# A seven-product scheme for part of the feed forward's first product

## The chip, the cores and the metric

The kernel runs on one core of a Trainium2 chip. The metric is the device time of one execution in microseconds; the kernel before takes 2246.73 us (median of 3 runs, 2246.26 to 2246.96).

## The reference, cut to what matters

Two transformer layers over 256 tokens of width 2048 in float32. The change is in the first layer's feed forward, whose hidden width is 5632:

```python
def swiglu(x, w_in, w_out):
    g, u = jnp.split(x @ w_in, 2, axis=-1)
    return (jax.nn.silu(g) * u) @ w_out
```

Here `w_in` is [2048, 11264], its left half the gate, its right half the up projection. Ahead of it stand a mixer and an attention over a memory, each with a residual and a layer norm; behind it a residual, a layer norm and the second layer.

## The kernel before, in words

Every large product is taken with TensorE in float32r. A float32 operand is written as the sum of a high part, the operand rounded to float32r, and a low part, the rest. `split` (L100) makes them: ScalarE copies to the high part (L101), VectorE subtracts it from the operand for the low part (L102). `mm3` (L121) takes a product as three matmuls: high by high (L124), activations' high by weights' low (L125), activations' low by weights' high (L126). The activations are stationary, one tile of 128 rows by 128 tokens; the weights move, 512 columns at a time, so one block of 128 rows by 512 columns costs three matmuls for each of the two token tiles.

`load_w` (L105) loads a chunk of weights in pieces of 2 blocks of 128 rows (128 x 1024 numbers, 512 KB) on SyncE's queue (SP, L112) into a `raw` tile, and splits it into a `hi` and a `lo` tile. Each of these pools has six tiles. `gemm_panels` (L128) goes through a panel of 512 columns block by block, both token tiles per block, and calls `evac` when a PSUM tile is complete.

The feed forward's first product is done by `ffn_in(j)` for j from 0 to 10 (L606 to L624). Each is a double panel: 512 columns of the gate, with silu on ScalarE (L611), then 512 columns of the up projection; VectorE multiplies (L619), and `to_pair` transposes the product with TensorE (L165) and splits it into `hT[j]`. For j = 0, the gain and offset of the second layer norm are applied to x (L556, L557) with bias tiles that GpSimd (POOL) loads (L93). The inner dimension of 2048 is 16 blocks of 128 rows. The second product follows in groups of 4, 4 and 3 double panels (L632), the first double panel of the next group being done ahead of it. PSUM's eight banks are 4 for products (`ps_g`), 2 for transposes (`ps_t`), 2 for attention (`ps_a`).

The kernel is written with a framework that sets the order of each engine's instructions and gives out the tiles of a pool at build time, by the order of the program and by when it reckons that an instruction is ready; on the chip each engine then runs its list in order. So a wait for a tile's release is a wait for the last reader of the tile before it.

Of the kernel before, what the change touches and what calls it, by code (L numbers as in the profile page):

```python
# [29 lines left out]
HEAD = 8  # L30
# [5 lines left out]
# columns of w_in  # L36
# [4 lines left out]
def build(ctx, tc, nc, a):  # L41
# [11 lines left out]
    stat = pool("stat", 4)  # L53
    ps_g = pool("ps_g", 4, PSUM)
    ps_t = pool("ps_t", 2, PSUM)
    ps_a = pool("ps_a", 2, PSUM)
# [20 lines left out]
    # token tile 1 sees 256 keys; the tables of tile 0 are the right halves of its  # L77
# [27 lines left out]
    def load_w(chunk_ap, kn, n, pieces=1):  # L105
        """One chunk of weights: kn blocks of 128 rows, n columns; hi and lo parts of each."""
        parts = []
        for k0 in range(0, kn, 2):
# [6 lines left out]
            for i in range(pieces):  # L115
                q = slice(2 * i // pieces, 2 * (i + 1) // pieces)
                split(raw[:, q, :], hi[:, q, :], lo[:, q, :])
# [36 lines left out]

    def acts_of(pairs):
        return [(h[:, i, :], l[:, i, :]) for h, l in pairs for i in range(4)]
# [4 lines left out]
    def transpose4(src):  # L161
        """src [128, 512] -> PSUM [128, 4, 128], each block of 128 columns transposed."""
        pt = ps_t.tile([128, 4, 128], F32, name="ps_t", tag="ps_t")
# [31 lines left out]
    def scores(q, k, tt, w):  # L195
        ps = ps_a.tile([128, 2, 256], F32, name="ps_a", tag="ps_a")
# [19 lines left out]
    def weigh(ps, v, causal_keys=True):  # L216
        """ps: per token tile [128, 2, 256]; v(i, sc) -> [128 keys, 128]. PSUM [128, 2, 256] = out^T."""
        o = ps_a.tile([128, 2, 256], F32, name="ps_a", tag="ps_a")
        for i in range(2):
            pt = ps_t.tile([128, 4, 128], F32, name="ps_t", tag="ps_t")  # L220
# [83 lines left out]
    kvg = const.tile([128, 256], F32, name="kvg")  # L304
    bcast_load(kvg, a["kv_norm_g"], 256)
    kig = const.tile([128, 64], F32, name="kig")
    bcast_load(kig, a["idx_k_norm_g"], 64)
    kib = const.tile([128, 64], F32, name="kib")
    bcast_load(kib, a["idx_k_norm_b"], 64)

    cTh = const.tile([128, 2, 256], F32R, name="cTh")
    cTl = const.tile([128, 2, 256], F32R, name="cTl")
# [3 lines left out]
    def ev_misc(tt, ps):  # L316
# [21 lines left out]
        pt = ps_t.tile([128, 4, 128], F32, name="ps_t", tag="ps_t")  # L338
# [17 lines left out]
    # keys of the memory  # L356
# [3 lines left out]
    # indexer scores and the choice of 64 keys  # L360
    mdsa = []
    for tt in range(2):
        w = 128 * (tt + 1)
        acc = later(f"score{tt}", FLOOR, tt=tt)
        for bp in range(4):
            # blocks 2 bp, 2 bp + 1 of two heads each; the heads of one row half share a bank
            for half in range(2):
                pr = slice(64 * half, 64 * half + 64)
                ps = ps_a.tile([128, 2, 256], F32, name="ps_a", tag="ps_a")
# [19 lines left out]
    # keys and values of the latent attention, per head  # L389
# [113 lines left out]
    # residual + layer norm  # L503
# [16 lines left out]
    # gains and offsets of the layer norms with one column per block of 128 of x's columns  # L520
# [380 lines left out]
def _lay_out(i):  # L901
    f = {k: np.asarray(v) for k, v in i.items()}
    w = f["w_in"][0]
    o = {}
# [58 lines left out]
```

## Time and profile before

| | |
|---|---|
| median of 3 runs | 2246.73 us |
| span of the profiled execution | 2244.9 us |
| TensorE busy | 2217.8 us (99%), 10080 matmuls |
| VectorE busy | 1278.9 us (57%) |
| ScalarE busy | 1056.4 us (47%) |
| mean granted TensorE clock | 0.997 of full speed |
| bytes moved by DMA | 423.96 MB, 189 GB/s on average |

The span runs from the first to the last instruction of the one execution that was profiled; the runs' own times lie 1.8 us above it. Times of instructions below are from that execution. Matmuls overlap in their pipeline, so the time from one start to the next counts, not the listed duration.

### The profile page before, as it was taken

Reading aid. Unit: us, or ns where it says so; the run is one execution under the profiler, and the core shown is the slowest. Engines: PE = TensorE matmul, PEld = TensorE weight load, DVE = VectorE, ACT = ScalarE, POOL = GpSimd, SP = SyncE. Lnnn points to the kernel's source line nnn. Section 1 sums busy time; section 2 is a strip of 40 time slices with the busy share of each in tenths; the row PEclk is TensorE's granted clock in tenths of the full one; section 3 lists DMA queues with packets and bytes.
Section 4 is the critical chain, followed back from the end, with each engine's and each line's share of the span. In section 5 each row is a group of like instructions: output and inputs, shape, how many; then the busy total and the mean of one; then the engine's idle time right before and its main releaser. Section 6 shows DMA issues by size and latency. Waiting matters only on the chain.

```text
span 2244.9 us, 26525 instructions
## 1 busy us (share of the span) xinstructions
PE 2217.8 (99%) x10080; PEld 1819.9 (81%) x10080; DVE 1278.9 (57%) x1563; ACT 1056.4 (47%) x1327; POOL 36.8 (2%) x75
## 2 busy tenths in 40 slices
PE   8999999999999999999999999999999999999999
PEld 6788888888887788888888888887788888888887
DVE  5666455555558774454455545467565565655553
ACT  5655445444435554443344434446555554444442
POOL 1000000000000000000000000001000000000000
PEclk9999999999999999999999999999999999999999
DMA  7654555656766375555555556557455556666563
GB/s 275 206 166 144 183 174 171 200 194 199 249 196 197 132 236 191 191 188 192 193 188 188 190 194 194 187 173 229 144 173 175 165 169 203 197 204 199 191 201 115
DMA packets 118480, 423.96 MB, mean 189 GB/s; under 512 B 13728, under 2 KB 14288, under 8 KB 118352
## 3 DMA queue, kind: packets, MB, share of 16 engines
q1 hardware_dynamic: 113760, 407.59, 55.2%
q0 software_dynamic: 4592, 14.68, 2.4%
q8 instruction: 79, 1.29, 0.2%
q14 instruction: 49, 0.40, 0.1%
HBM read 420.11 MB, written 2.10 MB: 188 GB/s over the span
## 4 chain that ended last, share of the span: by engine, by line
issue 66%; PE 30%; DMA 2%; POOL 1%; DVE 1%; ACT 0%; POOLq 0%; DVEq 0%; ACTq 0%
PE ps_g L125 9%; PE ps_g L126 9%; PE ps_g L124 9%; DMA bb<-ln_b 1%; PE ps_t L165 1%; DMA bb<-ln_g 1%; POOL bb L93 0%; DMA bb<-b_gate 0%; PE ps_a L198 0%; PE ps_a L232 0%; DVE lo L102 0%; PE ps_a L233 0%; ACT tmp L298 0%; PE ps_t L221 0%; PE ps_a L741 0%
## 5 line engine op out<-in xcount | busy, mean ns | idle before, releaser
L102 DVE TENSOR_TENSOR lo<-raw,hi 128x1024 fp32r<-128x1024 f32 (+2 forms) x766 | 931.7, 1218 | 874.7 <-ACT hi L101 873.7
L101 ACT CAST hi<-raw 128x1024 fp32r<-128x1024 f32 (+2 forms) x766 | 802.5, 1049 | 1038.4 <-PE ps_g L126 995.9
L125 PE MATMUL ps_g<-lo,hnTh 128*128 128x512 f32 x768 | 301.8, 393 | 2.3 <-DVE lo L102 2.3
L126 PE MATMUL ps_g<-hi,hnTl 128*128 128x512 f32 x768 | 302.1, 393 | 0.0
L124 PE MATMUL ps_g<-hi,hnTh 128*128 128x512 f32 x768 | 302.1, 393 | 0.0
L124 PE MATMUL ps_g<-hi,x2Th 128*128 128x512 f32 x704 | 275.0, 391 | 0.0
L126 PE MATMUL ps_g<-hi,x2Tl 128*128 128x512 f32 x704 | 274.8, 390 | 0.0
L125 PE MATMUL ps_g<-lo,x2Th 128*128 128x512 f32 x704 | 274.2, 390 | 0.0
L124 PE MATMUL ps_g<-hi,xTh 128*128 128x512 f32 (+1 forms) x608 | 236.5, 389 | 6.2 <-ACT hi L101 6.2
L125 PE MATMUL ps_g<-lo,xTh 128*128 128x512 f32 (+1 forms) x608 | 236.9, 390 | 1.5 <-DVE lo L102 1.3
L126 PE MATMUL ps_g<-hi,xTl 128*128 128x512 f32 (+1 forms) x608 | 237.8, 391 | 0.0
L125 PEld LDWEIGHTS ps_g<-lo,hnTh 128*128 128x128 f32 x768 | 145.1, 189 | 32.3 <-DVE lo L102 2.7
L124 PEld LDWEIGHTS ps_g<-hi,hnTh 128*128 128x128 f32 x768 | 145.2, 189 | 29.7 <-ACT crow L742 0.3
L126 PEld LDWEIGHTS ps_g<-hi,hnTl 128*128 128x128 f32 x768 | 144.9, 189 | 29.5
L125 PEld LDWEIGHTS ps_g<-lo,x2Th 128*128 128x128 f32 x704 | 132.2, 188 | 27.3 <-DVE lo L102 0.2
L124 PEld LDWEIGHTS ps_g<-hi,x2Th 128*128 128x128 f32 x704 | 132.2, 188 | 27.2 <-DVE x2Th L546 0.2
L126 PEld LDWEIGHTS ps_g<-hi,x2Tl 128*128 128x128 f32 x704 | 132.2, 188 | 27.1
L124 PEld LDWEIGHTS ps_g<-hi,xTh 128*128 128x128 f32 x608 | 114.7, 189 | 28.9 <-ACT hi L101 6.9
L126 PE MATMUL ps_g<-hi,hTl 128*128 128x512 f32 x352 | 137.3, 390 | 0.0
L124 PE MATMUL ps_g<-hi,hTh 128*128 128x512 f32 x352 | 137.2, 390 | 0.0
L125 PE MATMUL ps_g<-lo,hTh 128*128 128x512 f32 x352 | 136.9, 389 | 0.0
L125 PEld LDWEIGHTS ps_g<-lo,xTh 128*128 128x128 f32 x608 | 114.6, 188 | 25.6 <-DVE lo L102 3.4
(325 smaller groups left out, 2403.3 us busy)
## 6 DMA issues: line engine op xcount, KB each, us to landing
raw<-w_fi SPq DMA_DIRECT2D x176, 512.0 KB, 4.1
raw<-w_qkvg SPq DMA_DIRECT2D x96, 512.0 KB, 3.7
raw<-w_g SPq DMA_DIRECT2D x96, 512.0 KB, 4.4
raw<-w_fo SPq DMA_DIRECT2D x88, 512.0 KB, 3.7
raw<-w_out SPq DMA_DIRECT2D x64, 512.0 KB, 4.5
raw<-w_ga SPq DMA_DIRECT2D x32, 512.0 KB, 4.7
raw<-w_gb SPq DMA_DIRECT2D x32, 512.0 KB, 4.6
raw<-w_up SPq DMA_DIRECT2D x24, 512.0 KB, 4.6
```

What stands on the lines that cost most here:

```text
L101: nc.scalar.copy(hi, src)
L102: nc.vector.tensor_sub(lo, src, hi.bitcast(F32))
L124: nc.tensor.matmul(ps, ah[:, tok(tt)], wh, start=first, stop=False)
L125: nc.tensor.matmul(ps, ah[:, tok(tt)], wl, start=False, stop=False)
L126: nc.tensor.matmul(ps, al[:, tok(tt)], wh, start=False, stop=last)
L165: nc.tensor.transpose(pt[:, i, :], src[:, i * 128:(i + 1) * 128], ident)
```

## The change

For the double panels 1 to 10, gate and up projection are done together in `duo`. The 16 blocks of rows are eight pairs. With the two token tiles, the two blocks of a pair and the two panels, a pair is a product of 2 x 2 blocks by 2 x 2 blocks. For pairs 0, 1 and 2 (`FAST`) it is taken with seven block products instead of eight (`seven`): `sums_of` makes four sums of activation blocks once, VectorE makes four sums of weight blocks each time, and these are split as well. Four of the seven products are gathered in PSUM over the three pairs and combined by `combine` into an addend for each of the four results; the other three go directly into the results' PSUM tiles. The remaining five pairs are done as before (`eight`), the last two together, token tile by token tile. In pairs 4, 5 and 7 (`BY_DMA`) the up projection's low part comes another way: ScalarE writes minus the high part, and a DMA on POOL's queue adds the weights to it. The order of the pairs is `PLAN`. `to_pair` is put off to the next double panel, behind `combine`.

With that go: transposes and attention share four PSUM banks (`ps_m`), some constants move from their own tiles into the pool of `unit` tiles, and the second product goes in groups of 3, 3, 3 and 2 double panels.

```diff
+PLAN = (0, 3, 1, 4, 2, 5, 6, 7)
+FAST = (0, 1, 2)
+BY_DMA = (4, 5, 7)
+FFN_GROUPS = ((0, 3), (3, 6), (6, 9), (9, 11))
...
+    hi1s = pool("hi1s", 2)
+    lo1s = pool("lo1s", 2)
     ps_g = pool("ps_g", 4, PSUM)
-    ps_t = pool("ps_t", 2, PSUM)
-    ps_a = pool("ps_a", 2, PSUM)
+    ps_m = pool("ps_m", 4, PSUM)
...
+    def split_dma(src, hi, lo):
+        nc.scalar.copy(hi, src)
+        nc.scalar.mul(lo, src, -1.0)
+        nc.gpsimd.dma_start(lo, src, accum_op=OP.add)
+    def load_w(chunk_ap, kn, n, pieces=1, by=None):
...
-                split(raw[:, q, :], hi[:, q, :], lo[:, q, :])
+                (by or split)(raw[:, q, :], hi[:, q, :], lo[:, q, :])
...
+    def sums_of(pr, q):
+        full = tmps.tile([128, 2, 256], F32, name="sfull", tag="tmp")
+        nc.vector.tensor_add(full, pr[0][:, 2 * q:2 * q + 2, :].bitcast(F32), pr[1][:, 2 * q:2 * q + 2, :].bitcast(F32))
+        z = tmps.tile([128, 4, 128], F32, name="ssum", tag="tmp")
+        a11, a21 = full[:, 0, tok(0)], full[:, 0, tok(1)]
+        a12, a22 = full[:, 1, tok(0)], full[:, 1, tok(1)]
+        nc.vector.tensor_sub(z[:, 0, :], a21, a22)
+        nc.vector.tensor_sub(z[:, 1, :], z[:, 0, :], a11)
+        nc.vector.tensor_sub(z[:, 2, :], a11, a21)
+        nc.vector.tensor_add(z[:, 3, :], a12, z[:, 1, :])
+        u = unit([128, 2, 4, 128], F32R, "sums")
+        split(z, u[:, 0], u[:, 1])
+        return [(u[:, 0, i, :], u[:, 1, i, :]) for i in range(4)]
+    later_q = []
+    def flush():
+        while later_q:
+            later_q.pop(0)()
+    def mm3s(ps, act, w, first, last):
+        (ah, al), (wh, wl) = act, w
+        nc.tensor.matmul(ps, ah, wh, start=first, stop=False)
+        nc.tensor.matmul(ps, ah, wl, start=False, stop=False)
+        nc.tensor.matmul(ps, al, wh, start=False, stop=last)
+    def duo(w0, w1, evacs, acts, sums, plan):
+        n = 512
+        aps = [w0, w1]
+        P = [[ps_g.tile([128, n], F32, name="ps_g", tag="ps_g") for _ in range(2)] for _ in range(2)]
+        used = [[0, 0], [0, 0]]
+        fast = [i for i in plan if i in sums]
+        slow = [i for i in plan if i not in sums]
+        extra = len(fast)
+        total = [[2 * len(slow) + extra, 2 * len(slow) + extra], [2 * len(slow) + extra, 2 * len(slow)]]
+        N = {}
+        def at(i, k, tt):
+            h, l = acts[2 * i + k]
+            return h[:, tok(tt)], l[:, tok(tt)]
+        def block(p, i, k):
+            j = 2 * i + k
+            return aps[p][j // 4].rearrange("p (k n) -> p k n", n=n)[:, j % 4, :]
+        def into(tt, p, act, w):
+            used[tt][p] += 1
+            mm3s(P[tt][p], act, w, used[tt][p] == 1, used[tt][p] == total[tt][p])
+        def raw_tile():
+            return raws.tile([128, 2, n], F32, name="raw", tag="raw")
+        def two(src):
+            h = his.tile([128, 2, n], F32R, name="hi", tag="hi")
+            l = los.tile([128, 2, n], F32R, name="lo", tag="lo")
+            split(src, h, l)
+            return (h[:, 0, :], l[:, 0, :]), (h[:, 1, :], l[:, 1, :])
+        def seven(i):
+            ra, rb = raw_tile(), raw_tile()
+            nc.sync.dma_start(ra[:, 0, :], block(0, i, 0))
+            nc.sync.dma_start(rb[:, 0, :], block(1, i, 0))
+            nc.sync.dma_start(ra[:, 1, :], block(1, i, 1))
+            nc.sync.dma_start(rb[:, 1, :], block(0, i, 1))
+            t13, t24 = raw_tile(), raw_tile()
+            b11, b22 = two(ra)
+            nc.vector.tensor_add(t13, ra, rb[:, 0:1, :].to_broadcast([128, 2, n]))
+            t1, t3 = two(t13)
+            nc.vector.tensor_add(t24[:, 0, :], t13[:, 0, :], ra[:, 1, :])
+            h = hi1s.tile([128, n], F32R, name="hi1", tag="hi1")
+            l = lo1s.tile([128, n], F32R, name="lo1", tag="lo1")
+            split(rb[:, 1, :], h, l)
+            nc.vector.tensor_add(t24[:, 1, :], t24[:, 0, :], rb[:, 1, :])
+            t2, t4 = two(t24)
+            if not N:
+                for m in ("1", "5", "7", "6"):
+                    N[m] = ps_m.tile([128, n], F32, name="ps_m", tag="ps_m")
+            s1, s2, s3, s4 = sums[i]
+            a, z = i == fast[0], i == fast[-1]
+            mm3s(N["1"], at(i, 0, 0), b11, a, z)
+            mm3s(N["5"], s1, t1, a, z)
+            mm3s(N["7"], s3, t3, a, z)
+            into(0, 0, at(i, 1, 0), (h, l))
+            into(0, 1, s4, b22)
+            mm3s(N["6"], s2, t2, a, z)
+            into(1, 0, at(i, 1, 1), t4)
+        def eight(group):
+            w = {}
+            for i in group:
+                for p in range(2):
+                    ap = aps[p][i // 2].rearrange("p (k n) -> p k n", n=n)[:, 2 * (i % 2):2 * (i % 2) + 2, :]
+                    w[i, p] = load_w(ap, 2, n, by=split_dma if p == 1 and i in BY_DMA else None)
+            for tt in range(2):
+                for p in range(2):
+                    for i in group:
+                        for k in range(2):
+                            into(tt, p, at(i, k, tt), w[i, p][k])
+                    if used[tt][p] == total[tt][p]:
+                        finish(tt, p)
+        add = {}
+        def combine():
+            e0 = unit([128, 2, n], F32, "add")
+            e1 = unit([128, 2, n], F32, "add")
+            add[0, 0], add[0, 1], add[1, 0], add[1, 1] = e0[:, 0, :], e0[:, 1, :], e1[:, 0, :], e1[:, 1, :]
+            nc.scalar.copy(add[0, 0], N["1"])
+            nc.vector.tensor_add(add[1, 0], add[0, 0], N["6"])
+            nc.vector.tensor_sub(add[0, 1], N["5"], add[1, 0])
+            nc.vector.tensor_add(add[1, 0], add[1, 0], N["7"])
+            nc.vector.tensor_sub(add[1, 1], N["5"], add[1, 0])
+        def finish(tt, p):
+            if add:
+                nc.vector.tensor_add(add[tt, p], add[tt, p], P[tt][p])
+                evacs[p](tt, add[tt, p])
+            else:
+                evacs[p](tt, P[tt][p])
+        rest, flushed = list(plan), False
+        while rest:
+            i = rest.pop(0)
+            if i in sums:
+                seven(i)
+                if i == fast[-1]:
+                    combine()
+                    flush()
+                    flushed = True
+            elif len(rest) <= 1:
+                eight([i] + rest)
+                rest = []
+            else:
+                eight([i])
+                if not fast and not flushed:
+                    flush()
+                    flushed = True
...
-        pt = ps_t.tile([128, 4, 128], F32, name="ps_t", tag="ps_t")
+        pt = ps_m.tile([128, 4, 128], F32, name="ps_t", tag="ps_m")
...
+    norms = unit([128, 384], F32, "norms")
+    kvg, kig, kib = norms[:, 0:256], norms[:, 256:320], norms[:, 320:384]
...
+    x2S = {}
...
-        gemm(a["w_fi"][2 * j], x2A, ev_g, head=HEAD if j == 0 else 0)
         hT[j] = pair("hT")
         def ev_u(tt, ps):
             nc.vector.tensor_mul(sg[tt], sg[tt], ps)
-            to_pair(sg[tt], hT[j], tt)
-        gemm(a["w_fi"][2 * j + 1], x2A, ev_u)
+            later_q.append(lambda: to_pair(sg[tt], hT[j], tt))
         if j == 0:
+            gemm(a["w_fi"][0], x2A, ev_g, head=HEAD)
+            gemm(a["w_fi"][1], x2A, ev_u)
+            flush()
             ln_affine(1)
+            for i in FAST:
+                x2S[i] = sums_of(x2T[i // 2], i % 2)
+        else:
+            duo(a["w_fi"][2 * j], a["w_fi"][2 * j + 1], (ev_g, ev_u), x2A, x2S, PLAN)
...
-    groups = [range(0, 4), range(4, 8), range(8, 11)]
+    groups = [range(j0, j1) for j0, j1 in FFN_GROUPS]
...
             ffn_in(groups[gi + 1][0])
+        flush()
...
-    for gi, (k0, k1) in enumerate(((0, 2048), (2048, 4096), (4096, 5632))):
-        o[f"w_fo{gi}"] = _panels(fo[k0:k1])
+    for gi, (k0, k1) in enumerate(FFN_GROUPS):
+        o[f"w_fo{gi}"] = _panels(fo[512 * k0:512 * k1])
```

## Rows read from the trace of the kernel before

**Rows 1.** The page's first part: engine, busy us (share of span), instructions.

```profile
span 2244.9 us, 26525 instructions
...
PE 2217.8 (99%) x10080; PEld 1819.9 (81%) x10080; DVE 1278.9 (57%) x1563; ACT 1056.4 (47%) x1327; POOL 36.8 (2%) x75
```

**Rows 2.** Busy time in stretches: feed forward, double panels 1 to 3, double panel 0.

```profile
core 0: us, PE busy (x) PEld busy (x) DVE busy (x) ACT busy (x) POOL busy (x), PEclk, DMA share, GB/s
836.00:967.00 131.00, 131.00 (x591) 108.43 (x590) 64.78 (x59) 56.23 (x60) 0.00 (x0) 1.00 0.59 189
790.00:1512.00 722.00, 721.63 (x3232) 596.61 (x3230) 377.73 (x363) 305.50 (x320) 4.53 (x8) 1.00 0.59 193
792.86:836.00 43.14, 43.14 (x196) 35.70 (x195) 31.46 (x36) 19.65 (x22) 3.77 (x7) 1.00 0.78 265
```

**Rows 3.** Waits, 740 to 1540 us: who waited for whom, us, times, longest.

```profile
ACT hi L101 <- PE ps_g L126: 416.7, 254, 5.7
DVE lo L102 <- ACT hi L101: 345.2, 250, 3.0
...
PEld ps_t L165 <- DVE sg L619: 2.8, 11, 0.3
```

**Rows 4.** Timeline of PE: a matmul and the twelfth after it.

```profile
880.41 0.39 PE L124 MATMUL ps_g<-hi,x2Th 128*128 128x512 f32 x1
...
883.13 0.39 PE L124 MATMUL ps_g<-hi,x2Th 128*128 128x512 f32 x1
```

**Rows 5.** Timeline of ACT: the silu of two double panels that follow each other.

```profile
890.13 1.28 ACT L611 ACTIVATE sg<-ps_g 128x512 f32<-128x512 f32 x2 [0.98 <-PE ps_g L126]
...
934.63 1.28 ACT L611 ACTIVATE sg<-ps_g 128x512 f32<-128x512 f32 x2 [0.98 <-PE ps_g L126]
```

**Rows 6.** Groups of instructions, 740 to 1540 us: busy us, mean ns, idle before.

```profile
L102 DVE TENSOR_TENSOR lo<-raw,hi 128x1024 fp32r<-128x1024 f32 x280 | 342.2, 1224 | 345.3 <-ACT hi L101 345.2
L101 ACT CAST hi<-raw 128x1024 fp32r<-128x1024 f32 x283 | 298.5, 1056 | 418.1 <-PE ps_g L126 416.7 <-ACT prob L584 0.8 <-ACT hi L101 0.3
...
L619 DVE TENSOR_TENSOR sg<-sg,ps_g 128x512 f32<-128x512 f32 x22 | 14.1, 680 | 0.0
...
L101 ACT CAST hTh<-ps_t 128x512 fp32r<-128x512 f32 x22 | 12.8, 582 | 0.9
```

**Rows 7.** Timeline of DVE: start, us, instructions that follow without a gap.

```profile
792.86 5.84 DVE L102 TENSOR_TENSOR lo<-raw,hi 128x1024 fp32r<-128x1024 f32 x5
...
825.82 1.28 DVE L102 TENSOR_TENSOR hTl<-ps_t,hTh 128x512 fp32r<-128x512 f32 x2
```

**Rows 8.** SP's loads at line 112: ns of an issue, min/median/max.

```profile
L112 SPq DMA_DIRECT2D raw<-w_fi x176: 327/328/328, 740.7 to 1412.4; - x176
```

**Rows 9.** DMA issues of the whole run: count, KB each, median us to landing.

```profile
raw<-w_fi SPq DMA_DIRECT2D x176, 512.0 KB, 4.1
...
bb<-ln_g POOLq DMA_DIRECT2D x12, 256.0 KB, 5.6
bb<-ln_b POOLq DMA_DIRECT2D x12, 256.0 KB, 5.1
...
x<-x POOLq DMA_DIRECT2D x4, 512.0 KB, 11.1
out<-x SPq DMA_DIRECT2D x8, 256.0 KB, 4.0
...
raw<-w_qi SPq DMA_DIRECT2D x4, 256.0 KB, 5.7
...
rb<-rel POOLq DMA_DIRECT2D x1, 512.0 KB, 9.3
```

**Rows 10.** Timeline of POOL, 798 to 1523 us: first, sixth, last two.

```profile
799.60 0.54 POOL L93 DMA_DIRECT2D bb<-ln_g  x1 [8.27 <-DVE x L557]
...
812.21 0.54 POOL L93 DMA_DIRECT2D bb<-ln_b  x1 [0.67 <-DVE x L556]
816.36 0.54 POOL L93 DMA_DIRECT2D bb<-ln_g  x1 [3.61 <-DMA bb<-ln_g]
1521.00 0.54 POOL L93 DMA_DIRECT2D bb<-ln_b  x1 [704.11 <-DVE x L556]
```

**Rows 11.** Busy time in stretches: x being loaded, bias tiles being loaded.

```profile
586.00:590.00 4.00, 4.00 (x20) 3.30 (x19) 2.28 (x2) 1.25 (x2) 0.00 (x0) 1.00 1.03 414
805.00:815.00 10.00, 10.00 (x45) 8.26 (x44) 7.34 (x10) 3.77 (x4) 1.61 (x3) 1.00 0.78 261
```

More of the change, by code (lines that the diff above doesn't have):

```diff
@@ L102, in split @@
         nc.vector.tensor_sub(lo, src, hi.bitcast(F32))
-    def load_w(chunk_ap, kn, n, pieces=1):
+    def split_dma(src, hi, lo):
[3 more added lines that the diff above has]
+    def load_w(chunk_ap, kn, n, pieces=1, by=None):
         parts = []
@@ new lines, in build @@
+    later_q = []
[107 more added lines that the diff above has]
+                    flushed = True
+        return
@@ L195, in scores @@
     def scores(q, k, tt, w):
-        ps = ps_a.tile([128, 2, 256], F32, name="ps_a", tag="ps_a")
+        ps = ps_m.tile([128, 2, 256], F32, name="ps_a", tag="ps_m")
         for i in range(2):
@@ L216, in weigh @@
     def weigh(ps, v, causal_keys=True):
-        o = ps_a.tile([128, 2, 256], F32, name="ps_a", tag="ps_a")
+        o = ps_m.tile([128, 2, 256], F32, name="ps_a", tag="ps_m")
         for i in range(2):
-            pt = ps_t.tile([128, 4, 128], F32, name="ps_t", tag="ps_t")
+            pt = ps_m.tile([128, 4, 128], F32, name="ps_t", tag="ps_m")
             nc.tensor.transpose(pt[:, 0, :], ps[0][:, i, 0:128], ident)
@@ L302, in build @@
     xA = acts_of(xT)
-    kvg = const.tile([128, 256], F32, name="kvg")
+    norms = unit([128, 384], F32, "norms")
+    kvg, kig, kib = norms[:, 0:256], norms[:, 256:320], norms[:, 320:384]
     bcast_load(kvg, a["kv_norm_g"], 256)
-    kig = const.tile([128, 64], F32, name="kig")
     bcast_load(kig, a["idx_k_norm_g"], 64)
-    kib = const.tile([128, 64], F32, name="kib")
     bcast_load(kib, a["idx_k_norm_b"], 64)
-    cTh = const.tile([128, 2, 256], F32R, name="cTh")
-    cTl = const.tile([128, 2, 256], F32R, name="cTl")
+    cT = unit([128, 4, 256], F32R, "cT")
+    cTh, cTl = cT[:, 0:2, :], cT[:, 2:4, :]
     kidxT = const.tile([128, 256], F32, name="kidxT")
@@ L337, in ev_misc @@
                                            op0=OP.mult, op1=OP.add)
-        pt = ps_t.tile([128, 4, 128], F32, name="ps_t", tag="ps_t")
+        pt = ps_m.tile([128, 4, 128], F32, name="ps_t", tag="ps_m")
         for i in range(3):
@@ L368, in build @@
                 pr = slice(64 * half, 64 * half + 64)
-                ps = ps_a.tile([128, 2, 256], F32, name="ps_a", tag="ps_a")
+                ps = ps_m.tile([128, 2, 256], F32, name="ps_a", tag="ps_m")
                 for i in range(2):
@@ L701, in build @@
     pick = fb[:, 2:4, :].rearrange("p a (b c) -> p (a b) c", c=128)
-    ps = ps_a.tile([4, 256], F32, name="ps_a", tag="ps_a")
+    ps = ps_m.tile([4, 256], F32, name="ps_a", tag="ps_m")
     for tt in range(2):
@@ L705, in build @@
     nc.vector.tensor_copy(r3row, ps)
-    ps = ps_a.tile([4, 256], F32, name="ps_a", tag="ps_a")
+    ps = ps_m.tile([4, 256], F32, name="ps_a", tag="ps_m")
     for k in range(16):
@@ L728, in build @@
     for tt in range(2):
-        ps = ps_a.tile([128, 4], F32, name="ps_a", tag="ps_a")
+        ps = ps_m.tile([128, 4], F32, name="ps_a", tag="ps_m")
         nc.tensor.transpose(ps, fz[:, tok(tt)], ident[0:4, 0:4])
@@ L738, in build @@
     for hp in range(2):
-        ps = ps_a.tile([128, 2, 256], F32, name="ps_a", tag="ps_a")
+        ps = ps_m.tile([128, 2, 256], F32, name="ps_a", tag="ps_m")
         for i in range(2):
```

## The prediction, made before the changed kernel was run

> **What bounds the kernel now.** I read the page's busy times first [rows 1]: TensorE (PE) is busy for 2217.8 of 2244.9 us, VectorE (DVE) for 57% and ScalarE (ACT) for 47%. The stretches by stage [rows 2] put the feed forward at 790 to 1512 us, where PE never stops; in nearly three double panels (836 to 967 us) DVE works 64.78 of 131 us and ACT 56.23. The waits of this stage [rows 3] say the same from the other side: ACT waits for a matmul to free a high-part tile (416.7 us), DVE waits for ACT's high part (345.2 us), and PE's own waits are a few us (its weight loads wait 2.8 us for the products that are transposed). So only PE time counts here, as long as the others keep up. One matmul of 512 columns follows the last every 2.72 / 12 = 0.2267 us (twelve lie between the two lines of [rows 4]); its listed 0.39 us overlaps. The gate's silu comes every 934.63 - 890.13 = 44.50 us [rows 5]: 192 matmuls (43.53), which leaves 0.12 us for each of 8 transposes.
>
> **What is removed.** A fast pair takes 21 matmuls instead of 24. Three pairs in each of 10 double panels save 90 matmuls: 90 x 0.2267 = 20.4 us, from 44.5 to 42.5 us a double panel. It is on the path, since PE bounds. The stationary tiles of the sums are 128x128 like the others. The median of the runs is 2246.7, 1.8 above the span of the profile; I take differences off the median, so 2226.3 is the whole gain.
>
> **What DVE gets.** Alone a 128x1024 subtraction takes 1.224 us and a 128x512 one 0.68 [rows 6]; back to back the pitch is (5.84 - 1.22) / 4 = 1.155 and about 0.60 [rows 7]. A fast pair has three wide low parts and one wide addition, one narrow low part and two narrow additions: 4 x 1.155 + 3 x 0.60 = 6.42 us. Three make 19.3. The five slow pairs have ten low parts, of which three go to DMA: 7 x 1.155 = 8.1. Combining takes 4 narrow operations, finishing 4, the product with the gate 2, the low parts of hT 2: 12 x 0.60 = 7.2. Sum 34.5 us, or 37.6 by the lone durations, against 41.5 us of matmuls: 83 to 91%, from 22 us before. It fits in the order of the plan too: pieces 0, 3, 1, 4, 2 need 19.3 + 3 x 1.155 = 22.7 us of DVE and give PE 3 x 4.76 + 2 x 5.44 = 25.2. ACT gets thirteen wide copies or negations of slow pairs (13.7), three fast pairs of 3 x 1.056 + 0.58 (11.2), one copy of a product, two silus and two hT parts (2.9): 27.8 us, which PE hides.
>
> **What the two chains add.** Inside a fast pair the chain is addition, ACT copy, subtraction, twice. The six slots of raw and of hi now serve 22 and 19 tiles a double panel instead of 16 each. PE's demand leaves room, because a slot of hi is taken again only after the last matmul of the tile before it. Loads come in 12 pieces of 256 KB and 10 of 512 KB; SP's issues are 0.33 us each [rows 8], 22 of them 7.3 of 41.5 us. A 512 KB weight load lands after 4.1 us; the 256 KB rows from SP are 4.0 and 5.7 [rows 9]. Between no cost and 1 us a panel I take 0.2 (the load fits before the need by my count): 2 us in all.
>
> **The accumulating DMA** is the open price; the trace has none. First its deadline. From the start of a double panel PE takes 4.76, 5.44, 4.76, 5.44, 4.76, 5.44 and 10.88 us. Pair 4's up weights are the tenth of the 19 hi tiles; with six slots, in order of need, they get the fourth to come free, pair 3's gate weights, last used at 4.76 + 0.75 x 5.44 = 8.84. They are first needed at 14.96 + 1.36 = 16.32. That leaves 7.48 us; ACT's copy and negation take 2 x 1.056 and the handovers about 0.2, so 5.2 us remain from issue to landing. For pair 5 it is the same (19.04 to 26.52). Pair 7 has 9.52 us, 7.2 net. A later landing stops PE, which runs in order, once each for pairs 4 and 5. Behind a waiting accumulation on POOL's queue stand only the next ones: the bias tiles are loaded up to 816 and from 1521 us [rows 10], the wait in between is on a free tile and costs nobody.
>
> Its price by rows [rows 9]: below, the quickest median of 256 KB, 4.0 us from SP (no stall); above, four loads of x issued together, 11.1 us (5.9 + 5.9 + 3.9 late, 157 us in all), and the first of two loads of rb, 9.3. Nearest are single POOL transfers beside weight traffic: the bias tiles, 256 KB, 5.1 and 5.6. They are half as long, but read the destination of nothing; 256 KB at the 414 GB/s seen when the queues are full [rows 11] are 0.6 us. On the other side, they fell into stretches with the transfers' engines 0.78 busy at 261 GB/s, where the feed forward otherwise has 0.59. I take 5.5: 0.3 late, 20 times, 6 us. For this transfer DMA: Bandwidth & Descriptors (the Trainium skill, section Bandwidth) gives 6.15 us of DMA time for 1 MB issued from GpSimd; half of it and the fixed 2 us of that page make an estimate of 5.1 us, by which this term would be nothing and the sum 2229. No run here shows it.
>
> Does DVE hold POOL's transfers up? The bias loads issued from 799.60 to 812.21 us [rows 10] went out between subtractions and additions on DVE, at 0.54 us each. SBUF — State Buffer (the Trainium skill, section Who interferes with whom) says that a DVE copy or cast in a two-port mode keeps GpSimd from writing descriptors until it ends, and that an operation with two SBUF inputs does not. By that nothing changes here, since the new DVE work has two inputs throughout; were descriptors held for a whole DVE instruction, 1.2 us would come on top, which is the slow rival's price below.
>
> **Once, and elsewhere.** Three sums after the first double panel: 3 x 6 operations of at most 0.60 = 10.8 us of DVE, which is busy for 31.46 of 43.14 us there [rows 2]; 0 to 3, I take 1. One more group of second products: 8 additions more on DVE of 0.68, hidden by PE; what covered the group's last hT before (the next group's first panel) still stands. Transposes and attention now share four PSUM banks instead of two and two: outside the feed forward PE idles about 27 us in all [rows 1], so -3 to +4; I take 0. The row norms' constants move pools: nothing.
>
> Sum: 2246.7 - 20.4 + 6 + 2 + 1 = 2235.3.
>
> **The rivals.**
> - *The whole gain.* Accumulations land within 5.2 us and the chains cost nothing: 2226. For it: PE has no wait in this stage, and weight loads land in 4.1 us [rows 9]. Against it: POOL's medians are longer than SP's.
> - *DVE becomes the bound.* If DVE idles for ACT's copy of both sums in each fast pair, 2 x 1.1 x 3 = 6.6 us a panel come on top of its 37.6 by the lone durations: 44.2 against 42.5, 1.7 lost in each of 10 panels: 2226.3 + 17 + 3 = 2246, no change. For it: DVE already waits for ACT before nearly every low part [rows 3]. Against it: other low parts are ready then, and the order of an engine's instructions is laid out by readiness.
> - *The accumulating DMA is late.* Issue to landing takes 6.7 us: 1.5 us late at pairs 4 and 5, 3 us a double panel, 30 in all: 2246.7 - 20.4 + 30 + 3 = 2259, slower. The balance turns at 5.2 + 17.4 / 20 = 6.1 us. For it: the 512 KB transfers on POOL's queue have medians of 9.3 and 11.1 us [rows 9], and an accumulation reads twice; its transfers and the weights share the queues' engines, busy 0.59 already [rows 2]. Against it: those rows were issued in groups.
>
> **How the numbers follow.** My sum (2235) gets 0.48, the whole gain 0.13, DVE bound 0.13, a late DMA 0.26. A measurement of this kernel tells about 0.2% (4.5 us) from no change. The sum and the whole gain lie on the faster side: 0.61; DVE bound is the same: 0.13; slower 0.26. The likeliest case's own range is 2228 to 2243. The range over the cases begins at the whole gain, 2226, and ends at 2262, a DMA of 6.8 us; what is left out is mostly a slower DMA. The bounds above it (9.3 and 11.1) are from transfers that queue behind each other, so I leave them in the tail.
>
> **What would show it.** TensorE's instructions must fall by 90, to 9990. Right: silu every 42.5 to 43.3 us, PE's waits for the line of the accumulation under 1 us each, DVE near 35 us a double panel with waits for ACT of a microsecond or less, no group of PE waits for lo on DVE above a few us. The accumulating issues' median to landing decides: under 5.2 the whole gain, 6.1 or more a loss. If PE waits for lo of DVE in pairs 0, 1 and 2, DVE is the bound. If PE waits at the start of each double panel, the slots of hi run out, which I costed at 2 us.

## The result, and the profile after

The changed kernel takes 2287.13 us (median of 4 runs, 2281.91 to 2288.74) against 2246.49 us of the kernel before on the same chip: a ratio of 1.0179, 95% interval 1.0165 to 1.0193. It is slower by 40.6 us, where 11.4 us of gain were forecast; the time lies above the range. The profiled execution took 2286.14 us.

The page's first part [rows 1]:

```profile
span 2284.4 us, 26902 instructions
...
PE 2213.8 (97%) x9990; PEld 1810.8 (79%) x9990; DVE 1419.5 (62%) x1789; ACT 1134.1 (50%) x1430; POOL 62.5 (3%) x105
```

TensorE has its 90 matmuls less, and yet its busy time fell by only 4 us instead of 20.4; part of the matmuls ran at a lower clock, as shown below. The stretches of [rows 2], after:

```profile
836.00:967.00 131.00, 120.10 (x511) 96.77 (x510) 95.30 (x109) 73.82 (x85) 7.76 (x9) 0.96 0.73 210
790.00:1512.00 722.00, 685.51 (x2991) 557.79 (x2990) 498.52 (x567) 369.66 (x416) 30.31 (x38) 0.98 0.69 206
```

PE idles for 36.5 of 722 us in the feed forward (0.4 before), and the granted clock has fallen from 1.00 to 0.98. DVE is busy for 95.30 of the 131 us, so it isn't the bound. The waits from 740 to 1540 us [rows 3], after (waiting engine, tile and line, what ended it; us, times, longest):

```profile
DVE lo L110 <- ACT hi L109: 185.3, 132, 8.5
...
PEld ps_g L200 <- DMA lo<-raw: 42.1, 19, 4.9
ACT hi L109 <- DMA raw<-w_fi: 38.5, 24, 6.0
...
PE ps_g L200 <- DMA lo<-raw: 34.1, 17, 4.4
```

A new pair of lines stands there: PE's weight loads wait for the accumulating DMA 19 times, 2.2 us on average, and its matmuls 17 times. By the times of the issues, these 17 are pair 4 in all ten panels, pair 5 in five of them and pair 7 in two. The DMA issues of the whole run [rows 9]:

```profile
raw<-w_fi SPq DMA_DIRECT2D x116, 512.0 KB, 4.7
raw<-w_fi SPq DMA_DIRECT2D x120, 256.0 KB, 4.6
...
lo<-raw POOLq DMA_DIRECT2D x30, 512.0 KB, 6.7
```

One such case in the timeline of all engines, pair 4 of a double panel (start, us, engine, line; in brackets the idle time before it and who ended it):

```profile
892.88 2.00 ACT L109 CAST hi<-raw 128x1024 fp32r<-128x1024 f32 x2 [1.95 <-DVE raw L250]
...
894.79 1.04 ACT L114 CAST hi<-raw 128x1024 fp32r<-128x1024 f32 x1
...
895.74 1.06 ACT L115 ACTIVATE lo<-raw 128x1024 fp32r<-128x1024 f32 x1
...
897.08 0.85 POOL L116 DMA_DIRECT2D lo<-raw  x1 [27.55 <-ACT lo L115]
...
901.35 0.39 PE L199 MATMUL ps_g<-hi,x2Th 128*128 128x512 f32 x1
904.10 0.50 PE L200 MATMUL ps_g<-lo,x2Th 128*128 128x512 f32 x1 [2.37 <-DMA lo<-raw]
...
905.67 0.63 PE L199 MATMUL ps_g<-hi,x2Th 128*128 128x512 f32 x1
906.09 0.63 PE L200 MATMUL ps_g<-lo,x2Th 128*128 128x512 f32 x1
```

ACT makes the copies of a fast pair's sums first (892.88 to 894.88), then the copy and the negation of pair 4. The accumulation is issued at 897.08, 4.5 us before PE wants the low part at 901.58 (one pitch of 0.23 behind 901.35), and PE goes on 7.0 us after the issue. Over the ten panels the time from pair 4's issue to the start of PE's wait is 2.3 to 6.6 us, 4.6 on average. What follows runs slower: the pitch is 0.42 us (905.67 to 906.09) where it was 0.23. The stretches of 3 us show the clock (the third column from the end is the granted clock):

```profile
901.00:904.00 3.00, 0.74 (x4) 0.28 (x2) 1.90 (x3) 1.01 (x2) 0.00 (x0) 1.00 0.72 212
904.00:907.00 3.00, 2.90 (x9) 2.28 (x10) 2.36 (x2) 0.98 (x2) 0.00 (x0) 0.67 0.60 171
907.00:910.00 3.00, 3.00 (x12) 2.41 (x11) 0.00 (x0) 1.49 (x2) 0.00 (x0) 0.76 0.96 303
910.00:913.00 3.00, 3.00 (x15) 2.46 (x14) 0.84 (x1) 2.93 (x4) 0.85 (x1) 1.00 1.04 369
```

After 2.4 us of idling the granted clock drops from full speed (2.4 GHz) to a mean of 0.67 and 0.76, part of the time at the lower level (1.2 GHz), and is back 6 us later; behind another stall it is 0.50 from 871 to 874 us. It doesn't fall behind every stall: in stretches of 2 us through the whole feed forward, the clock is below full speed in seven places, behind seven of the 17 waits (1.8 to 4.4 us long), and not behind two others of 2.1 and 2.8 us. Together these seven cost 11.9 us (the time in them by the missing share of the clock).

The loss stands in two places. By the loads' first issues, the feed forward (first of w_fi to first of w_qkvg) takes 1524.5 - 748.3 = 776.2 us against 1481.3 - 740.7 = 740.6 before. And 8 us were already lost ahead of it: the first load of w_qm is issued at 146.7 us, before at 138.7.

### The profile page after: what moved, and what is told of

Its sections match the earlier page's. It is cut to its first block, busy times and chain, and to the rows that moved or that the text cites. A ratio compares the mean times of both kernels' runs of the same rounds, so it can differ in the third digit from the quotient of the medians.

```text
span 2284.4 us, 26902 instructions
## 1 busy us (share of the span) xinstructions
PE 2213.8 (97%) x9990; PEld 1810.8 (79%) x9990; DVE 1419.5 (62%) x1789; ACT 1134.1 (50%) x1430; POOL 62.5 (3%) x105
## 4 chain that ended last, share of the span: by engine, by line
PE 81%; DMA 8%; DVE 5%; issue 4%; ACT 1%; SPq 0%; POOL 0%; POOLq 0%; DVEq 0%; ACTq 0%
PE ps_g L139 22%; PE ps_g L140 22%; PE ps_g L138 22%; DMA lo<-raw 4%; DMA raw<-w_fi 3%; PE ps_g L200 3%; PE ps_g L201 3%; PE ps_g L199 3%; DVE lo L110 2%; PE ps_t L327 2%; PE ps_a L360 1%; PE ps_a L394 1%; ACT hi L109 1%; DMA memTraw<-memT 1%; DMA raw<-w_qi 0%
## 5 line engine op out<-in xcount | busy, mean ns | idle before, releaser
L110 DVE TENSOR_TENSOR lo<-raw,hi 128x1024 fp32r<-128x1024 f32 (+1 forms) x796 | 947.1, 1196 | 715.6 <-ACT hi L109 711.6
L109 ACT CAST hi<-raw 128x1024 fp32r<-128x1024 f32 (+1 forms) x796 | 813.8, 1032 | 936.7 <-PE ps_g L140 725.0
L200 PE MATMUL ps_g<-lo,x2Th 128*128 128x512 f32 x460 | 186.3, 405 | 34.2 <-DMA lo<-raw 34.1
L199 PE MATMUL ps_g<-hi,x2Th 128*128 128x512 f32 x460 | 184.0, 401 | 0.6 <-ACT hi L109 0.6
L201 PE MATMUL ps_g<-hi,x2Tl 128*128 128x512 f32 x460 | 183.9, 400 | 0.0
L200 PEld LDWEIGHTS ps_g<-lo,x2Th 128*128 128x128 f32 x460 | 88.8, 193 | 60.2 <-DMA lo<-raw 42.1
L140 PEld LDWEIGHTS ps_g<-hi,xTl 128*128 128x128 f32 x608 | 115.0, 189 | 22.9 <-issue 0.3
L199 PEld LDWEIGHTS ps_g<-hi,x2Th 128*128 128x128 f32 x460 | 89.1, 194 | 20.1 <-ACT hi L109 1.0
```

The lines of the kernel that those rows point to most:

```text
L109: nc.scalar.copy(hi, src)
L110: nc.vector.tensor_sub(lo, src, hi.bitcast(F32))
L140: nc.tensor.matmul(ps, al[:, tok(tt)], wh, start=False, stop=last)
L199: nc.tensor.matmul(ps, ah, wh, start=first, stop=False)
L200: nc.tensor.matmul(ps, ah, wl, start=False, stop=False)
L201: nc.tensor.matmul(ps, al, wh, start=False, stop=last)
```

## The experiments

The theory after the result: the accumulating DMA comes too late in each double panel, and costs PE's wait and the clock behind it. Rivals: the scheme itself costs (chains, DVE), or the shared PSUM banks do. The 8 us ahead of the feed forward need a cause of their own. No kernel below leaves out a part of the computation. Times are medians; each ratio is to the kernel before on the same chip, with its 95% interval.

**Parts apart.** Three kernels, by two constants of the changed kernel: without the DMA (the second edit below), without DMA and scheme (both), the DMA alone (the first):

```diff
-FAST = (0, 1, 2)
+FAST = ()
...
-BY_DMA = (4, 5, 7)
+BY_DMA = ()
```

> The changed kernel with no accumulating DMA: VectorE makes all low parts, the seven-product scheme stays. Theory A (the accumulating DMAs land too late; TensorE waits 42 us for them, and the granted clock is at its lower level for a while after): these waits and the dips of the clock in the feed forward go, and the time falls by 42 to 58 us, to 2229 to 2245. Theory B (VectorE is the bound of the scheme; its 35 us per double panel become 38): TensorE waits for VectorE's low parts instead, and the time stays above 2265. Theory C (sharing PSUM banks and moved constants): no change, 2287.

> The changed kernel with no fast pairs and no accumulating DMA; the shared PSUM banks, moved constants, pair order, late transposes and groups of 3, 3, 3, 2 stay. Theories A and B: TensorE has its 10080 matmuls again and waits for nothing in the feed forward; about 8 us are lost ahead of 150 us in the trace as in the changed kernel and about 4 won in the second layer: 2246 to 2255. Theory C: the loss is in what stays, so 2270 or more.

> The changed kernel with no fast pairs, but with the accumulating DMA in pairs 4, 5 and 7. Theory A, in the form that the deadline makes the DMA late and not the DMA as such: with two high tiles a pair a slot comes free three pairs ahead, 12 us before the need instead of 7.5, against 2 us on ScalarE and 6.7 us to land, so TensorE hardly waits: within 6 us of the kernel without scheme and DMA. If the DMA is late whatever the deadline (it delays weight loads, or waits in POOL's queue): 20 to 60 us more than that kernel.

Without the DMA: 2236.79 us, 0.9955 [0.9941, 0.9970]. Without DMA and scheme: 2249.62, 1.0014 [1.0005, 1.0024]. The DMA alone: 2255.95, 1.0041 [1.0026, 1.0056]. The first two came as expected; the third was expected within 6 us of the second or at least 20 above it, and is 6.3 above. So the three accumulations per double panel cost 2287.1 - 2236.8 = 50.3 us beside the scheme and 6.3 us without it; the scheme by itself gains 12.8. The stretches of the kernel without the DMA:

```profile
836.00:967.00 131.00, 130.46 (x585) 107.58 (x585) 115.80 (x131) 71.48 (x83) 0.00 (x0) 1.00 0.64 209
790.00:1512.00 722.00, 718.12 (x3216) 591.19 (x3215) 567.64 (x646) 364.53 (x419) 4.53 (x8) 1.00 0.60 196
```

PE is full again at full clock, with DVE at 88% of the three panels: DVE takes the three low parts that the DMA was to take from it, and PE hardly waits. The scheme and DVE aren't what costs. The whole feed forward, by the loads' first issues, without the DMA and in the changed kernel:

```profile
746.07:1472.85 726.78, 721.49 (x3230) 593.51 (x3229) 569.36 (x649) 371.39 (x429) 4.53 (x8) 1.00 0.59 194
748.25:1524.50 776.25, 737.34 (x3230) 599.77 (x3229) 536.05 (x619) 398.32 (x459) 30.31 (x38) 0.98 0.67 202
```

It is 49.5 us longer with the DMA, nearly all of the 50.3, for the same 3230 matmuls. PE idles 38.9 us instead of 5.3, which is 33.6 of it. Its matmuls take 15.9 us longer: 11.9 by the clock, and 4 that no row explains. In the kernel with the DMA alone the same transfer takes longer, 7.8 us, and yet PE's weight loads wait for it only 6.1 us in all. By the count of tiles there is more time: eight slow pairs of 5.44 us share 16 raw and 16 hi tiles a panel there, where with three fast pairs it is 22 and 19.

**The shared banks.** Products, transposes and attention in two and two banks again:

```diff
-    ps_m = pool("ps_m", 4, PSUM)
+    ps_t = pool("ps_t", 2, PSUM)
+    ps_a = pool("ps_a", 2, PSUM)
...
-                    N[m] = ps_m.tile([128, n], F32, name="ps_m", tag="ps_m")
+                    q, t = (ps_t, "ps_t") if m in "15" else (ps_a, "ps_a")
+                    N[m] = q.tile([128, n], F32, name="ps_m", tag=t)
```

> The changed kernel with two PSUM banks for transposes and two for attention again; the four products of the scheme take these four banks. If the sharing of banks costs the 8 us between 70 and 150 us of the trace: 2279, with the waits in the feed forward as they are. If the moved constants cost them: 2287, no change.

2299.79 us, 1.0228 [1.0203, 1.0254]: slower than the change by 12.7, which neither expectation had, and the early loss stays (first load of w_qm at 145.9 us). So the shared banks are not its cause. Where the 12.7 us come from isn't shown; the order of TensorE's instructions differs too.

**The constants.** The kernel without the DMA lost time early as well: its first load of w_qm is issued at 145.1 us, 6.4 us later than before. From 70 to 150 us, before and in this kernel:

```profile
70.00:150.00 80.00, 75.75 (x364) 60.17 (x363) 58.00 (x135) 41.57 (x65) 0.00 (x0) 1.00 0.53 177
70.00:150.00 80.00, 70.65 (x335) 56.42 (x334) 56.53 (x136) 42.19 (x66) 0.00 (x0) 0.94 0.50 169
```

PE's waits from 60 to 100 us name the place; before, only the first of them stood there, with 3.2 us:

```profile
PE ps_t L501 <- DVE cn L493: 5.6, 2, 4.0
...
PE ps_g L138 <- ACT memTh L109: 3.6, 1, 3.6
```

memTh is the high part of the memory. The memory's first load is issued at 55.4 us before and at 74.9 in the kernel without the DMA; its eight copies run at 60.6 to 80.4 us before, and here only from 82.3 to 100.5. The row norms' constants and the transposed constant `cT` hold two of the 25 unit tiles in which the memory is loaded. This kernel puts them into two small pools that idle at that time:

```diff
-    norms = unit([128, 384], F32, "norms")
+    norms = hi1s.tile([128, 384], F32, name="norms", tag="hi1")
-    cT = unit([128, 4, 256], F32R, "cT")
-    cTh, cTl = cT[:, 0:2, :], cT[:, 2:4, :]
+    cTh = hi1s.tile([128, 2, 256], F32R, name="cTh", tag="hi1")
+    cTl = lo1s.tile([128, 2, 256], F32R, name="cTl", tag="lo1")
```

> The kernel without accumulating DMA (2236.8), with the moved constants taken out of the unit tiles again and put into the pools hi1 and lo1, which stand empty that early. Theory (two unit tiles less make the second operand's load, memTraw, wait for a tile, and TensorE loses 8 us between 70 and 90 us of the trace): this stretch looks as before the change, and the time is 2228 to 2231. Rival (the loss is from the shared PSUM banks or the order of instructions): no change, 2236.

2227.89 us, 0.9912 [0.9896, 0.9928]: 8.9 us under the kernel without the DMA, and 18.6 under the 2246.49 of the kernel before (19.4 under the 2247.32 measured beside it). The first load of the memory is issued at 55.2 us again, that of w_qm at 136.4. The same stretch now:

```profile
70.00:150.00 80.00, 77.28 (x372) 62.94 (x372) 58.73 (x136) 42.55 (x65) 0.00 (x0) 0.98 0.53 181
```

**Which accumulations.** Two per double panel: on the late pairs 6 and 7 (in the changed kernel, and with the constants back), as below, or on the tight pairs with `(4, 5)`:

```diff
-BY_DMA = (4, 5, 7)
+BY_DMA = (6, 7)
```

> The changed kernel with accumulating DMA in pairs 6 and 7 alone, whose tiles come free 10.9 and 9.5 us before TensorE needs them, against 2.3 on ScalarE and 6.7 to land = 9.0. Theory A (deadline): hardly any wait for the DMA, 2234 to 2242, as without DMA. Rival (any such DMA costs about the same, by POOL's queue, ScalarE's negation or delayed weight loads): two thirds of the loss of 50 us stay, about 2270.

> The changed kernel with accumulating DMA in pairs 4 and 5 alone, whose tiles come free 7.5 us before the need. Theory A (deadline): they carry nearly all of the loss, 2275 to 2290. Rival (any such DMA costs the same): as with pairs 6 and 7, about 2270.

> The kernel with the constants out of the unit tiles, and the accumulating DMA in pairs 6 and 7. Theory A: within 4 us of the same without DMA (2228 to 2233); VectorE is 2.3 us lighter a double panel, which is worth something only where TensorE waits for it, 2 us in all by the trace of the kernel without DMA.

On pairs 6 and 7: 2250.62, 1.0015 [1.0005, 1.0025], with the constants back 2241.27, 0.9977 [0.9967, 0.9987]. On pairs 4 and 5: 2280.07, 1.0151 [1.0133, 1.0170]. Over their kernels without any these are 13.8, 13.4 and 43.3 us, though all three move as much. The waits for the accumulation from 790 to 1560 us, pairs 6 and 7:

```profile
PEld ps_g L200 <- DMA lo<-raw: 10.0, 11, 1.9
```

and pairs 4 and 5:

```profile
PEld ps_g L200 <- DMA lo<-raw: 35.3, 18, 3.1
```

The landing time is the same, 6.7 us in both. So the place in the panel sets most of the cost: pairs 4 and 5 came as the deadline had it (2275 to 2290). But pairs 6 and 7 lie above what the deadline gave (2234 to 2242, with the constants back 2228 to 2233) and under the rival's 2270: 13 us for pairs with room are more than PE's wait for them.

**A fourth fast pair**, with the constants back and no DMA; the sums need room, so second products go in smaller groups:

```diff
-PLAN = (0, 3, 1, 4, 2, 5, 6, 7)
-FAST = (0, 1, 2)
-FFN_GROUPS = ((0, 3), (3, 6), (6, 9), (9, 11))
+PLAN = (0, 4, 1, 5, 2, 6, 3, 7)
+FAST = (0, 1, 2, 3)
+FFN_GROUPS = ((0, 2), (2, 4), (4, 6), (6, 8), (8, 11))
```

> The kernel with the constants out of the unit tiles and no accumulating DMA (2227.9), with four fast pairs (order 0, 4, 1, 5, 2, 6, 3, 7; second products in groups of 2, 2, 2, 2, 3 so that the tiles suffice). Matmuls alone: 30 fewer, 6.8 us less, 2221. Theory (VectorE has 34.5 + 3.5 us a double panel with three fast pairs and no DMA, 4.1 more with four: 42.1 against 41.8 us of TensorE): VectorE becomes the bound, TensorE waits for its low parts, 2228 to 2245.

2237.43, 0.9956 [0.9941, 0.9971]: 30 matmuls less, and 9.5 us more than with three. PE's idling grew to 14.8 us of 722 (5.1 with three), in waits for DVE's additions and low parts. That fits the expectation that DVE becomes the bound, but it isn't shown: the control of the traffic below, with three fast pairs, the same smaller groups and a few tiles less, loses more, 13.8 us.

**Accumulations earlier.** Load, copy, negation and DMA of the next slow pair go ahead of the pair before it, in the changed kernel and in the one with the constants back:

```diff
+        ready = {}
+        def early(i):
+            ap = aps[1][i // 2].rearrange("p (k n) -> p k n", n=n)[:, 2 * (i % 2):2 * (i % 2) + 2, :]
+            ready[i] = load_w(ap, 2, n, by=split_dma)
...
             i = rest.pop(0)
+            for q in rest if len(rest) == 2 else rest[:1]:
+                if q in BY_DMA and q not in ready:
+                    early(q)
```

> The changed kernel with the same three accumulating DMAs a double panel, but their load, copy and DMA are set ahead of the piece before them, so that their tiles are taken from the six one piece earlier (by my count 16 us before TensorE's need in pairs 4 and 5 instead of 7.5). Nothing else is changed. Theory A (deadline): the waits for the DMA fall from 42 us to under 8, the clock stays at its upper level in the feed forward, 2236 to 2246. Rival (these DMAs cost what they cost wherever they stand, or the tiles taken early starve the fast pairs): over 2262.

> The same early accumulating DMAs, with the constants out of the unit tiles. Theory A: 8 us less than with the constants in them, 2228 to 2238, so no better than without any DMA (2227.9), where VectorE kept up.

2285.94, 1.0174 [1.0157, 1.0191], and 2277.89, 1.0139 [1.0123, 1.0156]. PE now never waits for an accumulation, and nothing is won; both were expected at 2246 or less by the deadline, and the rival (over 2262) has it. The waits of the first of them, 790 to 1560 us:

```profile
ACT hi L109 <- DMA raw<-w_fi: 103.7, 51, 5.1
...
PEld ps_t L336 <- DVE add L292: 17.0, 6, 4.6
PE ps_t L336 <- DVE add L292: 15.6, 6, 4.4
PEld ps_g L200 <- DVE lo L110: 11.4, 7, 3.0
```

The loss has moved: ACT waits 103.7 us for weight loads (38.5 in the changed kernel). Of the load queue's own waits, in the second of them, the two for `lo<-raw` are new against the kernel without the DMA:

```profile
SPq L126 <- DVE lo L110: 340.1, 138, 9.8
SPq L126 <- DMA lo<-raw: 70.0, 14, 8.5
...
SPq L238 <- DMA lo<-raw: 38.3, 10, 8.5
```

SP waits 70.0 + 38.3 us for raw tiles that an accumulation still reads, and issues in order, so every later load waits with it. Such waits don't cost anything by themselves. In the kernel with the DMA alone they are 233.9 us and the whole DMA costs 6.3; in the changed kernel they are 94.7, and there PE's own waits are almost all for the accumulations. They cost where the loads have no time to spare. The refined theory: a low part by DMA holds its raw tile (and its hi and lo tile) for the transfer as well, and that delays the loads behind it.

**More tiles.** One raw tile more, and, in another kernel, one hi and one lo tile more, on the kernel with the accumulations earlier and the constants back. SBUF is full, so each has a control with the same sacrifices (groups as for the fourth fast pair, 24 unit tiles; for the second also five tmp and two bias tiles). The first edit is one kernel, the second the other:

```diff
-N_R = 6
+N_R = 7
...
-N_W = 6
+N_W = 7
```

> As the kernel with the constants back and accumulations issued one piece earlier, with second products in groups of 2, 2, 2, 2 and 3, 24 unit tiles, and seven raw tiles instead of six. If what costs time is that a piece by DMA holds its raw tile for some 9 us instead of 2.3, one tile more gives room for part of it: ACT's waits for loads of the feed forward's weights fall from about 100 us by a third or more, and the time is at least 8 us below that of the same kernel with six raw tiles. If the transfers themselves are what is short (DMA engines shared by weights and accumulations), or the chain by way of ACT, DMA and PE, the extra tile changes nothing: within 4 us of the kernel with six.

> The control for the kernel with seven raw tiles: the same groups of second products and 24 unit tiles, six raw tiles. Both theories expect near 2278 us (between 2270 and 2288), and ACT's waits for loads of the feed forward's weights near 100 us between 790 and 1560 us.

> As the control (constants back, accumulations one piece earlier, second products in groups of 2, 2, 2, 2 and 3, 24 unit tiles, five tmp and two bias tiles) with seven hi and seven lo tiles instead of six. If a piece by DMA costs time because it holds its hi and lo tiles some 7 us longer, this gives part of it back: at least 8 us under the control. If tiles are not what is short, it stays within 4 us of the control.

> The control for seven hi and lo tiles: like the kernel with six raw tiles, with five tmp tiles and two bias tiles. Expected 2276 to 2290 us by every theory.

Seven raw tiles 2290.09, 1.0202 [1.0185, 1.0219], control 2281.37, 1.0167 [1.0145, 1.0189]. Seven hi and lo tiles 2323.83, 1.0336 [1.0317, 1.0356], control 2292.34, 1.0201 [1.0186, 1.0217]. Neither theory had that: 8.7 and 31.5 us slower. The second control is itself just above the 2276 to 2290 expected of it. Another number of tiles is another order as well, since tiles and orders are given out at build time; in the kernel with seven hi and lo tiles the order of TensorE itself differs from its control's. With seven raw tiles it is the same. There SP waits for accumulations even longer (108.3 and 54.6 us; 82.2 and 44.9 in its control), and ACT's waits for loads are 112.1 us (102.6). These four runs don't settle it.

**The traffic alone.** The kernel with the constants back, no low part by DMA, but at the same 30 places an accumulation into a scratch tile; its control is without:

```diff
+    def traffic(src):
+        s = scr_s[turn[0] % 2]
+        turn[0] += 1
+        nc.scalar.mul(s[:, 0, 0:1], src, -1.0)
+        nc.gpsimd.dma_start(scr_d, s.to_broadcast([128, 2, 512]), accum_op=OP.add)
...
+                    if p == 1 and i in TRAFFIC:
+                        traffic(w[i, p][0][0][:, 0:1].bitcast(F32))
```

> No low part by DMA: all are subtracted by VectorE. At the same 30 places an accumulating DMA of 512 KB on POOL's queue adds one scratch tile to another, and nothing waits for it but the next of its kind; ScalarE gives the start by one column per piece. If the transfers' share of the DMA engines is what costs, the time is at least 15 us above the same kernel without them. If it is the way of a piece through ScalarE, the queue and PE, in order, with its tiles held, it stays within 5 us.

> The control for the traffic alone: constants back, no low part by DMA, second products in groups of 2, 2, 2, 2 and 3, 24 unit tiles, five tmp and two bias tiles. Expected 2226 to 2236 us by every theory (2227.9 with 25 unit tiles and groups of 3).

2252.93, 1.0025 [1.0016, 1.0034], against 2241.65, 0.9977 [0.9965, 0.9989] for the control, which is itself slower than the 2226 to 2236 expected of it (the smaller groups and fewer tiles cost 13.8 us over 2227.9). The traffic costs 11.3 us, between the two expectations: a real share, but less than a quarter of the 50.3. It isn't quite the same traffic: these transfers, which read a scratch row twice, land after 9.6 us instead of 6.7. In the traffic kernel ACT's waits for weight loads are 34.6 us, 14.6 in the control.

**Out of HBM.** Like the kernel with the constants back and accumulations earlier, but the DMA adds the weights from HBM, and the raw tile is free after ACT's two passes:

```diff
-        nc.gpsimd.dma_start(lo, src, accum_op=OP.add)
+        nc.gpsimd.dma_start(lo, far, accum_op=OP.add)
...
-                (by or split)(raw[:, q, :], hi[:, q, :], lo[:, q, :])
+                (by or split)(raw[:, q, :], hi[:, q, :], lo[:, q, :], *([chunk_ap[:, k0 + q.start:k0 + q.stop, :]] if by else []))
```

> As the kernel with the constants back and accumulations one piece earlier (2277.9 us), except that the accumulating DMA adds the weights out of HBM instead of out of the raw tile, so a piece by DMA gives its raw tile back after ScalarE's copy and negation. TensorE's order is the same. If the held raw tile, and SP's queue that waits for it in order, make most of the loss, SP's waits for accumulations (108 us there) go, ACT's waits for weight loads fall from 102 us to under 60, and the time falls by 15 us or more, to below 2263. If the DMA engines' load makes it, or the lo tile's lateness, the time stays within 6 us or rises, since HBM traffic is added.

2257.46, 1.0050 [1.0033, 1.0067]: 20.4 us under the kernel that reads the raw tile, TensorE's order being the same. The transfers take longer and cost less; its DMA issues:

```profile
raw<-w_fi SPq DMA_DIRECT2D x116, 512.0 KB, 5.3
raw<-w_fi SPq DMA_DIRECT2D x120, 256.0 KB, 5.7
lo<-w_fi POOLq DMA_DIRECT2D x30, 512.0 KB, 9.0
```

The queue's waits for accumulations are gone (its longest are now for DVE's low parts, as before the change). ACT's wait for weight loads is smaller:

```profile
ACT hi L109 <- DMA raw<-w_fi: 75.0, 43, 6.4
```

It was 102.4 with the raw tile held. That is not under the 60 expected, but the time is under its 2263. So the held raw tile with the in-order load queue makes 20.4 of the 50.0 us (2277.89 - 2227.89) that earlier accumulations cost, net of the longer transfers; the traffic's 11.3, measured apart in another kernel, would leave some 18 if the two add up. Held hi and lo tiles, ScalarE's negations and the different order are left for these; no run shows which.

## Why the prediction was wrong

**What bounds the kernel** held: PE's time counts, and each of its waits is seen in the end.

**What is removed**: 90 matmuls went. Where the DMA doesn't disturb them, the seven-product panels are shorter nearly by what was worked out: the gate's silu [rows 5] in the kernel with the constants back,

```profile
861.45 0.63 ACT L774 ACTIVATE sg<-add 128x512 f32<-128x512 f32 x1
...
904.20 0.63 ACT L774 ACTIVATE sg<-add 128x512 f32<-128x512 f32 x1
```

42.75 us apart instead of 44.50, where 42.5 were forecast (the next comes after 43.18). In the changed kernel two of them stand at 877.71 and 925.20, 47.5 apart. Over the whole feed forward the scheme gave a little less than its terms: without any accumulation it takes 726.8 us with the scheme and 741.6 without, 14.8 less, where 20.4 - 3 were forecast.

**What DVE gets** held: 34.5 us a panel by the pitches, and the changed kernel has 95.30 / 131 x 47.4 = 34.5 (two spacings of its silu are 972.43 - 877.71 = 94.7). With three low parts more it still fits (115.80 of 131 us). So the rival in which DVE becomes the bound is out, and the DMA relieves an engine that didn't need it.

**What the two chains add**: 2 us were taken. Without the DMA PE idles 3.9 of the 722 us; the size is right. But "the load fits before the need by my count" held only there, where each raw tile comes back after a copy and a subtraction, 2.3 us by [rows 6]. With an accumulation reading it, ACT waits longer for loads: 38.5 us against 25.4.

**The accumulating DMA** is the step that failed: the term of 6 us measured 50.3. The late rival had the right sign, and its 6.7 us from issue to landing were the measured median; none of the prediction's rows had that number, so that it came out exactly is luck. The step went wrong in four places.

- The price was taken as 5.5 us and was 6.7 (4.8 to 9.2).
- The room was 4.5 us in the case shown and not 5.2, because ACT first copied a fast pair's sums: the deadline was worked out from the hi slot alone, and ACT's order was left out. With 0.7 us less room, the rival's 1.5 us a wait become the 2.2 that were seen. The waits are 42 us by weight loads and 34 by matmuls, where the rival had 30. Its count of 20 came out near 19 in part by luck, since pair 5 waited only half the time, and pair 7 twice.
- The fall of the clock behind some of the stalls, 11.9 us, was in neither the sum nor the rival.
- The question was only when the DMA lands. That it also holds tiles, on which the loads wait in order, was not among the terms. In the kernels with earlier accumulations PE never waits for one and the loss is as large; 20.4 us of that loss are the held raw tile, by the run out of HBM, and the cause of the rest stays open.

The estimate from the Trainium skill, DMA: Bandwidth & Descriptors, section Bandwidth, 5.1 us, is below the measured 6.7. That page of the Trainium skill gives its figure for a load out of HBM. The sum by it, 2229, is close to the time without any accumulation, which is another matter. Of the rule from the Trainium skill, SBUF — State Buffer, section Who interferes with whom (a DVE operation with two SBUF inputs doesn't keep POOL from writing descriptors), the trace agrees as far as it goes: the 30 accumulations issue in 0.85 to 0.91 us, no longer where DVE is at work than where it isn't.

**Once, and elsewhere**: "The row norms' constants move pools: nothing" was wrong by 8.9 us. Two tiles come out of the pool into which the memory is loaded at that time. The shared banks were no loss that any run shows. With the constants back and no DMA, 2227.89 us is near the sum without the DMA's term, 2229.3, but partly by luck: by the loads' first issues its feed forward is 11.6 us shorter than before (729.0 against 740.6), and 4.4 us are gained outside it, which the sum had at nothing and no run explains.

**What would show it**: the prediction named the median to landing as what decides, with 6.1 as the turn. The sign came out by it, at 6.7. But the same 6.7 cost 13.8 us in pairs 6 and 7 and 43.3 in pairs 4 and 5, so the median alone doesn't decide.

## What to carry to other kernels

Moving work to a DMA frees an engine and lengthens the life of every tile that the work touches: count the tiles per period, who waits in order for them, and whether those loads have time to spare, before asking when the transfer lands. Relieve only an engine that the trace shows short; DVE at 88% of these panels still kept up. A constant that takes a tile from a rotating pool costs what the pool's busiest moment loses by it.

## What was not expected of the hardware

An accumulating DMA of 512 KB from SBUF to SBUF lands after 6.7 us beside the weight loads (7.8 in the kernel with the DMA alone), and 9.0 out of HBM; a weight load of the same size takes 4.7. Its issue takes POOL 0.85 us, where a plain load took 0.54 [rows 10]. After the PE stall of 2.4 us shown above the granted clock had a mean of 0.67 over the next 3 us, and it fell so behind seven of the 17 stalls; these cost more than their own length.
